# A two-layer attention trunk on one core: PSUM reads ordered behind a bank's matmuls, query halves placed by transfers, and a new issue order

## The chip, the core and the metric

The kernel runs on one core of one Trainium2 chip. Its engines run side by side, each through its own list of instructions in order: TensorE (PE, with its weight loads shown apart as PEld) multiplies matrices into PSUM, VectorE (DVE) and ScalarE (ACT) work element by element and can read PSUM, GpSimd (POOL) takes small powers, and SyncE (SP) issues the transfers. The metric is the time of one execution on the device in microseconds (us); smaller is better.

## The reference, cut to what matters

Two decoder layers over 512 tokens of width 1024, in float32. Layer 0 runs two attentions beside each other; layer 1 two others. After each layer a gated embedding is added.

```python
for i in range(2):
    h = _rms_norm(x, norm_gain[i])
    if i == 0:
        aq, ak, av, iq, ik, iw, ag, bq, bk, bv, bg = _split(h @ w_in, EVEN_SPLITS)
        # A: an indexer scores all causal keys (iq, ik, iw), each query keeps the best 128
        #    and attends to them with 8 heads (aq) on one key head
        # B: window of 128 keys, 8 heads (bq) on 2 key heads, a learned sink per head
        y = concat([attend_A * silu(ag), attend_B * silu(bg)]) @ w_out
    else:
        cq, ck, cv, cg, dq, dk, dv, dg = _split(h @ w_in, ODD_SPLITS)
        # C: dilated attention, D: difference of two softmax maps with an RMS norm per head
        y = concat([attend_C * silu(cg), attend_D * silu(dg)]) @ w_out
    x = x + y
    gate = sigmoid(_rms_norm(x, ple_norm_gain[i]) @ w_ple_gate[i])
    x = x + (p[i] @ w_ple_proj[i]) * gate
```

Queries and keys are normalised per head and rotated (`iq` is rotated only).

## The kernel before

**Products in two parts.** A float32 product is made of three matmuls on rounded parts (`PASSES`): high by high, high by low, low by high. `hilo` makes the parts: a cast on ACT writes the high part, a subtraction on DVE the low part. Weights come by a transfer into one of four `raw` buffers and are split into one of eight `w2` buffers (`weights`, `split_w`). `proj_tok` runs a projection: 8 pieces of 128 input rows, 3 passes, 4 tiles of 128 tokens, each tile into a PSUM bank of its own (`mm`, four banks). `evacuate` then empties the banks.

**Queries of layer 0.** `head_evac` scales and rotates a tile of queries, turns it with four transposes into the bank `tk`, and `put_stacked` writes it to two tensors. Even heads lie in partitions 0 to 63 of the turned bank and odd heads in 64 to 127. The first tensor holds the even heads, the high part in the lower half and the low part in the upper half of the partitions; the second holds the odd heads, with the halves the other way round. So one matmul over 128 rows takes both parts of a query at once. `put_stacked` runs for three tiles of the indexer's queries `iq` (the first needs none) and four each of `bq` and `aq`.

**Attention of layer 0.** `scores` multiplies a query tile with the keys, `exp_rows` adds the mask, finds the row's extreme on DVE and exponentiates on ACT. `attend_four` handles four heads of one query tile. Its probabilities are turned (`probs_t`) and multiplied with the values into the one bank `ob`, a column block of 128 for each head; `put_y` then reads the bank in two halves of partitions, two column blocks each, on ACT (or DVE, where the gate is multiplied in at once). `select` keeps the best 128 keys by repeated maxima on DVE.

**Layer 1.** `attend_d` collects the four heads of one query tile in the bank `ob`, and `finish_d` takes the square of each head's block on ACT, one instruction a head, before it scales the whole bank on DVE.

**The order.** The instructions aren't issued in the order in which the code names them. `Program.add` collects them with a price (`_price`) and with what each depends on: earlier instructions that touch the same part of a tile, columns of a bank in PSUM included (`_region`). `order` then runs through an imagined time, with a latency from engine to engine (`LATENCY`), and on each engine always takes the ready instruction of the lowest rank. The rank is the place in the code less a lead; `LEADS` lists a lead for each call of a decorated function (`@nc.part`). Transfers are priced by their bytes, in one queue. `issue` writes the instructions in the order that results.

In the profile every instruction stands under line 273, the call in `issue`; so tiles tell the groups apart. A name such as `ob<-pt,Ve` gives what is written and what is read. `slot` stands for all large tensors, queries and keys and the gated outputs among them; `sk` is a bank of scores, `tk` a bank of transposes, `pr` a row of probabilities, `pt` the turned ones, `pw` the stored product of the embedding, `t` a scratch tile and `tiny` a small one.

Of the kernel before, what the change touches and what calls it, by code (L numbers as in the profile page):

```python
# [21 lines left out]
P = 128  # L22
# [9 lines left out]
    "att": (34, -15, -766, -398, 669, 588, -77, -21, 2, 2, -149, -357, 50, 0, 7, 0, -82, -39, -2, 0, 30, 15, 0, 3,  # L32
# [6 lines left out]
    "idx": (1, -20, -4),  # L39
    "mm": (-20, 10, 0, -43, 0, -64, 152, 90, 1, 224, 32, -17, 67, -92, -33, -44, -226, 0, -5, 55, -26, -29, 207, -105,  # L40
         -78, 0, -70, -24, 0, -1013),
    "norm": (54, -1, 44, 0, 0, 0, 3, -51, 184, -234, 155, -150, -144, 161, 0, -203, 12, -2, -4, -232, 186, -87, 0, 0),
    "rows": (88, -835),
    "ss": (212, 408, 29, -8, 332, 193, 0, -1, -40, 0, -36, 98, 3, -61, 0, 337, 0, 2, 0, 33, 172, -17, -59, 3, 106, 28,
         378, -8, -232, 0, 0, -90),
    "tab": (880, -60, 139, -139, -289, -486),
    "top": (1, 0, -372, -1080, 138, -26, -16, -711, 22, -43, -305, -1922),
    "w": (-3, 80, 32, 111, -1, 0, 135, 10, 450, -45, -94, 0, -49, 0, -1, 13, -7, 0, 299, -31, -34, -26, 20, 32, 0, -1,
         0, 31, 9, 123),
    "x": (-355, 29),  # L50
    "y": (-697, -48, -1871, 13, 52, 122, 0, 3, -51, 11, 306, 0, -35, 6, -396, 0),
    None: 53,
# [4 lines left out]
SWITCH = 200  # L57
PR = 8
TOPK = 128
# [17 lines left out]
class Program:  # L77
# [9 lines left out]
    def _kept(ap):  # L87
# [5 lines left out]
               ("vector", "gpsimd"): 165, ("scalar", "gpsimd"): 185, ("vector", "vector"): 125, ("scalar", "scalar"): 140,  # L93
# [33 lines left out]
    def _price(self, engine, method, reads, writes):  # L127
        n = max([self._elements(x) for x in writes] + [self._elements(x) for x in reads if x.space != DRAM] + [1])
        if method == "dma_start":
            return 450  # L130
        if engine == "gpsimd":
            if n > 8:
                return 156 + 2.2 * n
            return 400 + 172 * n if method == "tensor_tensor" else 450
        psum = any(x.space == PSUM for x in reads)
        half = writes[0].ap[0][1] == 64
        pointers = sum(self._elements(x) == 1 for x in reads) if n > 1 else 0
        if engine == "scalar":
            return (58 if psum else 98) + 0.834 * n + 93 * (pointers + len(writes) - 1) + 122 * half
        if engine == "vector":  # L140
            fast = method == "tensor_scalar" and not psum
            return 72 + (0.52 if fast else 1.042) * n + 61 * pointers + 97 * half + 62 * (method == "match_replace")
        n = self._elements(writes[0])
        if method == "transpose":
            return 109
        if reads[0].dtype == BF16:
            return 427
        if reads[0].dtype == F32R:
            return max(109, 0.455 * n)
        return 218 / 128 * n  # L150
# [10 lines left out]
    def add(self, engine, method, args, kw):  # L161
# [22 lines left out]
        found = [(self._region(x), w) for w, xs in ((False, reads), (True, writes)) for x in xs]  # L184
        for (name, p0, p1, at), w in found:
            for j, v, q0, q1, there in self.touched.setdefault(name, []):
                if (w or v) and p0 < q1 and q0 < p1 and not at.isdisjoint(there):
                    after.add(j)
# [88 lines left out]
def tile_trunk(ctx: ExitStack, tc: tile.TileContext, a: dict, out: bass.AP):  # L277
# [123 lines left out]
    def proj_tok(pieces_n, evac, tiles=range(NT), order="kt", act=None, swap=0, cut=False):  # L401
# [5 lines left out]
        def mms(t, i, c0=0, c1=n):  # L407
            kt, w2 = pieces[i]
            for c, (xa, wa) in enumerate(PASSES):
                nc.tensor.matmul(banks[t][:, c0:c1], act[kt ^ (4 * swap)][:, xa, t * P:(t + 1) * P], w2[:, wa, c0:c1],  # L410
                                 start=(i == 0 and c == 0), stop=(i == last and c == 2))
        if order == "kt":
            for t in tiles:
                banks[t] = mm_bank()
            for i in range(last + 1):
                for t in tiles:
                    mms(t, i)
# [132 lines left out]
    def put_stacked(dst, t, bank):  # L550

        bv = bank.rearrange("p (k n) -> p k n", k=4)
        for j, d in enumerate(dst):
            own, other = [slice(64 * i, 64 * i + 64) for i in (j, 1 - j)]
            d = d[:, :, t * P:(t + 1) * P]
            hilo(d[own], d[other], bv[own])
# [86 lines left out]
    def attend_four(qb, key0, qT, kv, g, V, mask, y0, sink=None):  # L643
        nkb = qb + 1 - key0
        n = nkb * P
        nm, den, r = [tiny(4, tag=x, bufs=3) for x in ("nm", "den", "r")]
# [7 lines left out]
        if sink is not None:  # L654
            es = tiny(4, tag="es", bufs=3)
# [146 lines left out]
    proj_tok(wiq, head_evac(iqT, (cs, sn), rs0, normed=False, put=put_stacked), tiles=(1, 2, 3))  # L802
# [314 lines left out]
```

## Time and profile before

| | us |
|---|---|
| median of 3 runs | 685.43 |
| lowest and highest | 685.33, 685.48 |
| profiled execution | 685.89 |
| its span, first to last instruction | 684.1 |
| TensorE busy | 672.8 |
| DVE busy | 521.5 |
| ACT busy | 424.9 |
| POOL busy | 69.9 |

The span is that of the profiled execution; the time around it (1.8 us) is the rest of that execution. Busy times are sums over the span. Matmuls are pipelined and their ends are modelled, so TensorE's busy time includes part of its short waits.

### The profile page before, as it was taken

The numbers are of one execution on the slowest core, as the hardware profiler recorded it, in microseconds if no ns is written. First come the engines' busy times: TensorE is split into PE (matmuls) and PEld (weight loads), VectorE is DVE, ScalarE is ACT, GpSimd is POOL, SyncE is SP. The second block draws the span as 40 slices with busy tenths as digits, with TensorE's granted clock in tenths as the row PEclk, the third lists the DMA queues.
The fourth block names the chain that finished last, engine by engine and source line by source line (L and its number), as shares of the span: only waits on it lengthen the run. The fifth ranks groups of instructions, "written<-read, shape, count | busy, mean of one in ns | idle before, by whom it ended". The sixth has DMA issues, their size and how long they took to land.

```text
span 684.1 us, 10327 instructions
## 1 busy us (share of the span) xinstructions
PE 672.8 (98%) x3494; PEld 542.6 (79%) x3494; DVE 521.5 (76%) x1236; ACT 424.9 (62%) x968; POOL 69.9 (10%) x55
## 2 busy tenths in 40 slices
PE   9999999999999999999999999999999999999997
PEld 5888787788888888888778877777887877788886
DVE  6799999999998954554479389988699688755462
ACT  6767588889897763445456256767467565664341
POOL 0120221000010000100123031001141000000000
PEclk9999999999999999999999999999999999999999
DMA  9714131535221332232443322113024034132231
GB/s 334 290 46 139 47 93 45 159 92 164 98 63 32 121 115 74 78 130 95 131 130 114 96 62 78 47 61 108 17 77 144 13 109 138 47 106 64 77 124 46
DMA packets 37652, 68.45 MB, mean 100 GB/s; under 512 B 5216, under 2 KB 6624, under 8 KB 37344
## 3 DMA queue, kind: packets, MB, share of 16 engines
q1 hardware_dynamic: 37456, 67.79, 31.2%
q8 instruction: 27, 0.44, 0.3%
q14 instruction: 25, 0.20, 0.1%
q10 hardware_dynamic: 144, 0.02, 0.0%
HBM read 61.49 MB, written 6.30 MB: 99 GB/s over the span
## 4 chain that ended last, share of the span: by engine, by line
PE 89%; ACT 4%; DVE 3%; DMA 2%; issue 1%; SPq 0%; ACTq 0%; DVEq 0%
PE mm L273 68%; PE ob L273 8%; PE sk L273 8%; PE tk L273 6%; ACT pr L273 1%; DMA raw<-in_w_in_odd_dram 1%; DVE t L273 1%; DVE slot L273 1%; ACT slot L273 1%; DMA slot<-in_xT_dram 1%; ACT w L273 1%; DVE w L273 1%; DMA raw<-in_w_in_even_dram 0%; ACT t L273 0%; ACT pt L273 0%
## 5 line engine op out<-in xcount | busy, mean ns | idle before, releaser
L273 PE MATMUL mm<-w,AT 128*128 128x512 f32 (+2 forms) x1728 | 433.3, 398 | 0.4 <-DVE w L273 0.3
L273 PEld LDWEIGHTS mm<-w,AT 128*128 128x128 f32 x1728 | 312.2, 188 | 67.9 <-DVE w L273 1.6
L273 PE MATMUL mm<-AT,w 128*128 128x512 f32 x384 | 105.4, 405 | 0.0
L273 ACT ACTIVATE w<-raw,gains 128x512 fp32r<-128x512 f32 x96 | 67.8, 721 | 50.1 <-PE mm L273 41.4
L273 POOL TENSOR_TENSOR tiny<-tiny,mhalf 128x8 f32<-128x8 f32 (+1 forms) x32 | 59.5, 1864 | 372.1 <-DVE tiny L273 371.5
L273 DVE SCALAR_TENSOR_TENSOR w<-raw,gains,w 128x512 fp32r<-128x512 f32 x96 | 70.3, 746 | 34.5 <-ACT w L273 34.2
L273 PEld LDWEIGHTS mm<-AT,w 128*128 128x128 f32 x384 | 68.1, 189 | 12.8 <-issue 0.9
L273 ACT ACTIVATE pr<-pr,nm 128x256 f32<-128x256 f32 (+3 forms) x128 | 68.6, 538 | 15.5 <-DVE nm L273 15.1
L273 ACT CAST w<-raw 128x512 fp32r<-128x512 f32 x79 | 47.5, 619 | 22.6 <-PE mm L273 17.2
L273 PE MATMUL sk<-slot,slot 128*128 128x256 f32 (+7 forms) x368 | 61.1, 332 | 0.1
L273 DVE TENSOR_TENSOR w<-raw,w 128x512 fp32r<-128x512 f32 x80 | 54.2, 683 | 8.3 <-ACT w L273 8.2
L273 PEld LDWEIGHTS sk<-slot,slot 64*128 64x128 f32 (+1 forms) x368 | 42.9, 187 | 15.1 <-issue 3.6
L273 PE MATMUL tk<-ident,pr 128*128 128x128 f32 x256 | 44.7, 275 | 0.1
L273 PE MATMUL ob<-pt,Ve 128*128 128x128 f32 x272 | 39.6, 280 | 3.0 <-ACT slot L273 2.3
L273 PEld LDWEIGHTS ob<-pt,Ve 128*128 128x128 f32 x272 | 35.0, 191 | 8.8 <-ACT pt L273 3.6
L273 ACT CAST slot<-tk 64x512 fp32r<-64x512 f32 (+1 forms) x42 | 24.5, 583 | 23.2 <-PE tk L273 22.1
L273 DVE CUSTOM_DVE_ANT_0 pr<-sk,cpack 128x128 f32<-128x128 f32 (+3 forms) x72 | 31.5, 461 | 7.8 <-PE sk L273 7.5
L273 PEld LDWEIGHTS tk<-ident,pr 128*128 128x128 f32 x256 | 31.3, 141 | 7.5 <-ACT pr L273 1.4
L273 ACT COPY pt<-tk 128x512 f32<-128x512 f32 (+3 forms) x56 | 27.4, 490 | 13.0 <-PE tk L273 12.5
L273 DVE TENSOR_TENSOR t<-raww,tab 128x512 f32<-128x512 f32 x48 | 32.1, 681 | 4.0 <-ACT raww L273 3.8
L273 DVE TENSOR_TENSOR slot<-slot,mm 128x512 f32<-128x512 f32 x32 | 21.3, 684 | 16.3 <-PE mm L273 16.2
L273 DVE SCALAR_TENSOR_TENSOR t<-t,slot 128x512 f32<-128x512 f32 (+1 forms) x17 | 11.2, 659 | 29.3 <-ACT t L273 29.3
(98 smaller groups left out, 787.0 us busy)
## 6 DMA issues: line engine op xcount, KB each, us to landing
raw<-in_w_in_odd_dram SPq DMA_DIRECT2D x64, 256.0 KB, 2.7
raw<-in_w_in_even_dram SPq DMA_DIRECT2D x36, 256.0 KB, 3.1
raw<-in_w_ple_gate_dram SPq DMA_DIRECT2D x32, 256.0 KB, 3.0
slot<-in_x_dram SPq DMA_DIRECT2D x16, 256.0 KB, 6.3
raw<-in_w_out_even_dram SPq DMA_DIRECT2D x16, 256.0 KB, 2.8
raw<-in_w_out_odd_dram SPq DMA_DIRECT2D x16, 256.0 KB, 2.6
raw<-in_w_ple_proj_dram SPq DMA_DIRECT2D x8, 256.0 KB, 2.8
pw<-t SPq DMA_DIRECT2D x8, 256.0 KB, 3.5
```

Of the source, the lines that this page charges most:

```text
L273: getattr(getattr(nc, engine), method)(*args, **kw)
```

## The change

- **Reads of PSUM** (`Program.add`): an instruction of any engine but TensorE that touches a PSUM tile counts as touching all of it. Before, only the columns and partitions that it names counted.
- **Queries of layer 0** (`put_stacked`): the high and the low part of a tile are made on all 128 partitions at once, in two new buffers `qh` and `ql` (two each); four transfers, each of 64 partitions, carry the halves to their places.
- **First piece** (`proj_tok(..., first=True)`, used for `iq`): for the first piece of weights the passes run over all tiles in turn, and the pass with the weights' low part comes last.
- **Prices**: a power on POOL 500 + 185 n ns instead of 400 + 172 n, the latency from DVE to POOL 400 instead of 165 ns, a matmul 0.456 instead of 0.455 ns a column.
- **Buffers**: the small tiles `nm`, `den`, `r` and `es` of `attend_four` are two deep instead of three.
- **Order**: all entries of `LEADS` are new (cut here).

```diff
@@ -29,33 +29,36 @@
 BIG = 1.0e30
 GONE = -3.0e38
 LEADS = {
...
-    None: 53,
+    None: 62,
 }
 VECS = ("a_q_gain", "a_k_gain", "idx_k_gain", "b_q_gain", "b_k_gain", "c_q_gain", "c_k_gain", "d_q_gain", "d_k_gain",
         "d_lambda_q1", "d_lambda_k1", "d_lambda_q2", "d_lambda_k2")
 CPACK = 1792
 SWITCH = 200
+WHOLE = frozenset(range(512))
 PR = 8
+QB = 2
 TOPK = 128
 IDX_SCALE = 512.0 ** -0.5
 LAMBDA_INIT = 0.8 - 0.6 * math.exp(-0.3)
@@ -90,7 +93,7 @@
     ENGINES = ("tensor", "vector", "scalar", "gpsimd", "sync")
     LATENCY = {("scalar", "vector"): 140, ("scalar", "tensor"): 160, ("vector", "scalar"): 125, ("vector", "tensor"): 170,
                ("tensor", "scalar"): 210, ("tensor", "vector"): 215, ("gpsimd", "vector"): 80, ("gpsimd", "scalar"): 90,
-               ("vector", "gpsimd"): 165, ("scalar", "gpsimd"): 185, ("vector", "vector"): 125, ("scalar", "scalar"): 140,
+               ("vector", "gpsimd"): 400, ("scalar", "gpsimd"): 185, ("vector", "vector"): 125, ("scalar", "scalar"): 140,
                ("gpsimd", "gpsimd"): 120, ("tensor", "tensor"): 0}
 
     def __init__(self, tc):
@@ -131,7 +134,7 @@
         if engine == "gpsimd":
             if n > 8:
                 return 156 + 2.2 * n
-            return 400 + 172 * n if method == "tensor_tensor" else 450
+            return 500 + 185 * n if method == "tensor_tensor" else 450
         psum = any(x.space == PSUM for x in reads)
         half = writes[0].ap[0][1] == 64
         pointers = sum(self._elements(x) == 1 for x in reads) if n > 1 else 0
@@ -146,7 +149,7 @@
         if reads[0].dtype == BF16:
             return 427
         if reads[0].dtype == F32R:
-            return max(109, 0.455 * n)
+            return max(109, 0.456 * n)
         return 218 / 128 * n
 
     @contextmanager
@@ -182,6 +185,8 @@
             self.extra[i] = 7000 if any(list(x.ap)[-1][1] == 1 or list(x.ap)[-1][0] > 1 for _, x in aps) else 0
         after = self.after[i]
         found = [(self._region(x), w) for w, xs in ((False, reads), (True, writes)) for x in xs]
+        if engine != "tensor":
+            found = [((r[0], 0, P, WHOLE), w) if x.space == PSUM else (r, w) for (r, w), x in zip(found, reads + writes)]
         for (name, p0, p1, at), w in found:
             for j, v, q0, q1, there in self.touched.setdefault(name, []):
                 if (w or v) and p0 < q1 and q0 < p1 and not at.isdisjoint(there):
@@ -398,15 +403,16 @@
         evac(t, bank, *columns)
 
     @nc.part("mm")
-    def proj_tok(pieces_n, evac, tiles=range(NT), order="kt", act=None, swap=0, cut=False):
+    def proj_tok(pieces_n, evac, tiles=range(NT), order="kt", act=None, swap=0, cut=False, first=False):
         pieces, n = pieces_n
         act = [AT[:, :, kt, :] for kt in range(NK)] if act is None else act
         banks = {}
         last = len(pieces) - 1
 
-        def mms(t, i, c0=0, c1=n):
+        def mms(t, i, c0=0, c1=n, passes=range(3)):
             kt, w2 = pieces[i]
-            for c, (xa, wa) in enumerate(PASSES):
+            for c in passes:
+                xa, wa = PASSES[c]
                 nc.tensor.matmul(banks[t][:, c0:c1], act[kt ^ (4 * swap)][:, xa, t * P:(t + 1) * P], w2[:, wa, c0:c1],
                                  start=(i == 0 and c == 0), stop=(i == last and c == 2))
         if order == "kt":
@@ -414,7 +420,12 @@
                 banks[t] = mm_bank()
             for i in range(last + 1):
                 for t in tiles:
-                    mms(t, i)
+                    if i or not first:
+                        mms(t, i)
+                if first and not i:
+                    for c in (0, 2, 1):
+                        for t in tiles:
+                            mms(t, i, passes=(c,))
             for t in tiles:
                 evacuate(evac, t, banks[t])
         else:
@@ -549,11 +560,13 @@
 
     def put_stacked(dst, t, bank):
 
-        bv = bank.rearrange("p (k n) -> p k n", k=4)
+        hi, lo = [sb.tile([P, 4, P], F32R, name=uid(x), tag=x, bufs=QB) for x in ("qh", "ql")]
+        hilo(hi, lo, bank.rearrange("p (k n) -> p k n", k=4))
         for j, d in enumerate(dst):
             own, other = [slice(64 * i, 64 * i + 64) for i in (j, 1 - j)]
             d = d[:, :, t * P:(t + 1) * P]
-            hilo(d[own], d[other], bv[own])
+            nc.sync.dma_start(out=d[own].bitcast(F32), in_=hi[own].bitcast(F32))
+            nc.sync.dma_start(out=d[other].bitcast(F32), in_=lo[own].bitcast(F32))
 
     def head_evac(dst, tab, rs, normed=True, put=put_heads):
         def evac(t, bank):
@@ -643,7 +656,7 @@
     def attend_four(qb, key0, qT, kv, g, V, mask, y0, sink=None):
         nkb = qb + 1 - key0
         n = nkb * P
-        nm, den, r = [tiny(4, tag=x, bufs=3) for x in ("nm", "den", "r")]
+        nm, den, r = [tiny(4, tag=x, bufs=2) for x in ("nm", "den", "r")]
         prs = []
         for p in (2 * g, 2 * g + 1):
             for j, bank in enumerate(scores(qT, kTe, p, qb, key0, n, kv)):
@@ -652,7 +665,7 @@
                 init = 3.0e38 if sink is None else sink[0][:, h:h + 1]
                 prs.append(exp_rows(bank, n, mask[:, :n], init, nm[:, i:i + 1], den[:, i:i + 1]))
         if sink is not None:
-            es = tiny(4, tag="es", bufs=3)
+            es = tiny(4, tag="es", bufs=2)
             nc.vector.tensor_tensor(out=es, in0=nm, in1=sink[1][:, 4 * g:4 * g + 4], op=ALU.add)
             nc.scalar.activation(out=es, in_=es, func=AF.Exp)
             nc.vector.tensor_tensor(out=den, in0=den, in1=es, op=ALU.add)
@@ -799,7 +812,7 @@
         norm_scale(t, rs0)
 
     iqT = heads()
-    proj_tok(wiq, head_evac(iqT, (cs, sn), rs0, normed=False, put=put_stacked), tiles=(1, 2, 3))
+    proj_tok(wiq, head_evac(iqT, (cs, sn), rs0, normed=False, put=put_stacked), tiles=(1, 2, 3), first=True)
     wsmall = split_w(([(kt, wsm[kt // 4][:, kt % 4, :456]) for kt in range(NK)], 456))
     ktab = slot([P, 4, T]).rearrange("p a (b h d) -> p (a b) h d", b=2, h=4).rearrange("p (u t) h d -> p u t h d", u=2)
     for i, (gname, sc) in enumerate((("a_k_gain", 8.0), ("idx_k_gain", 8.0 * IDX_SCALE), ("b_k_gain", 8.0),
```

## Rows read from the trace of the kernel before

**Rows 1.** The page, busy time of each engine, share of the span and instructions.

```profile
PE 672.8 (98%) x3494; PEld 542.6 (79%) x3494; DVE 521.5 (76%) x1236; ACT 424.9 (62%) x968; POOL 69.9 (10%) x55
```

**Rows 2.** Busy time by stretch: length, then each engine's us, granted clock, transfers.

```profile
75.00:135.00 60.00, 58.89 (x317) 47.65 (x316) 57.44 (x158) 48.02 (x118) 12.48 (x6) 1.00 0.32 93
135.00:200.00 65.00, 64.45 (x385) 54.09 (x384) 63.28 (x199) 57.45 (x160) 3.96 (x2) 1.00 0.34 106
...
240.00:320.00 80.00, 79.36 (x402) 64.80 (x401) 40.73 (x71) 37.80 (x75) 2.74 (x5) 1.00 0.31 99
```

**Rows 3.** The bank `ob`: who waited for it, us in total, times.

```profile
PEld ob L273: 5.7, 9
...
PE ob L273: 3.9, 8
```

**Rows 4.** The timeline of `ob`: start, length, instruction, [idle before it, releaser].

```profile
95.13 1.05 PE L273 MATMUL ob<-pt,Ve 128*128 128x128 f32 x8
...
109.31 0.94 PE L273 MATMUL ob<-pt,Ve 128*128 128x128 f32 x6
...
110.28 0.38 ACT L273 ACTIVATE slot<-ob 64x256 f32<-64x256 f32 x1 [0.49 <-PE ob L273]
...
110.72 0.49 PE L273 MATMUL ob<-pt,Ve 128*128 128x128 f32 x2 [0.47 <-ACT slot L273]
...
578.59 0.61 PE L273 MATMUL ob<-slot,pt 128*128 128x128 f32 x4
...
579.74 0.49 PE L273 MATMUL ob<-slot,pt 128*128 128x128 f32 x2 [0.55 <-ACT t L273]
```

**Rows 5.** Groups by shape: count, busy us, mean ns, idle before.

```profile
L273 DVE TENSOR_TENSOR slot<-tk,slot 64x512 fp32r<-64x512 f32 x22 | 15.2, 689 | 4.8 <-ACT slot L273 4.4
...
L273 DVE TENSOR_TENSOR slot<-tk,slot 128x512 fp32r<-128x512 f32 x20 | 13.7, 683 | 0.8 <-ACT slot L273 0.7
...
L273 ACT CAST slot<-tk 64x512 fp32r<-64x512 f32 x22 | 12.8, 581 | 5.9 <-PE tk L273 4.9 <-DVE slot L273 0.8
...
L273 ACT CAST slot<-tk 128x512 fp32r<-128x512 f32 x20 | 11.7, 586 | 17.2 <-PE tk L273 17.2
```

**Rows 6.** The timeline near 119 us: a query's second cast, matmuls of an embedding product.

```profile
119.07 0.58 ACT L273 CAST slot<-tk 64x512 fp32r<-64x512 f32 x1 [0.80 <-DVE slot L273]
...
120.32 0.97 PE L273 MATMUL mm<-w,w 128*128 128x512 f32 x3 [0.63 <-ACT t L273]
```

**Rows 7.** The timeline of two query tiles and of the scores that follow.

```profile
40.41 1.39 DVE L273 TENSOR_TENSOR slot<-tk,slot 64x512 fp32r<-64x512 f32 x2 [0.24 <-ACT slot L273]
...
54.12 0.40 PE L273 MATMUL sk<-slot,slot 128*128 128x256 f32 x2
...
84.31 1.18 ACT L273 CAST slot<-tk 64x512 fp32r<-64x512 f32 x2 [2.46 <-PE tk L273]
...
85.52 1.41 DVE L273 TENSOR_TENSOR slot<-tk,slot 64x512 fp32r<-64x512 f32 x2 [0.33 <-ACT slot L273]
...
86.26 0.51 PE L273 MATMUL sk<-slot,slot 128*128 128x256 f32 x2
```

**Rows 8.** Transfers by kind (KB each, median us to landing), and one issue.

```profile
pw<-t SPq DMA_DIRECT2D x8, 256.0 KB, 3.5
...
out_dram<-slot SPq DMA_DIRECT2D x2, 128.0 KB, 1.8
...
124.63 0.39 SPq L273 DMA_DIRECT2D pw<-t  x1
```

**Rows 9.** The timeline of SP's queue: eight weight loads.

```profile
53.61 22.54 SPq L273 DMA_DIRECT2D raw<-in_w_in_even_dram  x8
```

**Rows 10.** The timeline of TensorE at the start.

```profile
6.07 1.47 PEld L273 LDWEIGHTS mm<-w,AT 128*128 128x128 f32 x7 [0.35 <-DVE w L273]
...
10.58 2.60 PE L273 MATMUL mm<-w,AT 128*128 128x512 f32 x10 [0.30 <-DVE w L273]
```

**Rows 11.** Groups by shape: the powers on POOL.

```profile
L273 POOL TENSOR_TENSOR tiny<-tiny,mhalf 128x8 f32<-128x8 f32 x24 | 50.8, 2121 | 280.8 <-DVE tiny L273 280.8
```

More of the change, by code (lines that the diff above doesn't have):

```diff
@@ L31 @@
 LEADS = {
-    "att": (34, -15, -766, -398, 669, 588, -77, -21, 2, 2, -149, -357, 50, 0, 7, 0, -82, -39, -2, 0, 30, 15, 0, 3,
[6 rows of a table removed]
[L39 to L51, printed above, removed]
-    None: 53,
+    "att": (-392, -476, -265, 55, 575, -382, 44, 15, -6, -149, -341, -446, -4, -57, 63, -14, 2, 2, -287, 388, 0, 0,
[7 rows of a table added]
+    "idx": (-5, -2, 0),
+    "mm": (15, 0, 153, 0, 10, -336, -84, 2, 8, 4, 0, -30, 30, -5, 88, -12, -304, 0, 41, 13, 136, -25, 206, -141, -135,
+         -6, -996, -1930, -2303, -10383),
+    "norm": (-3, -2, 0, -170, 60, -38, 0, -13, 142, 15, 0, -227, 0, -49, 15, -1, 0, 0, -396, -7, 21, 0, 0, -1844),
+    "rows": (0, 898),
+    "ss": (-64, 0, 0, 340, 576, 4, -39, 1269, 0, 0, -74, 119, 196, 55, 333, 112, -4, 45, -250, -182, 70, 0, 0, 1, 14,
+         -119, 0, 74, 0, 1, 0, -88),
+    "tab": (279, 13, -4, 0, -137, -2),
+    "top": (193, -101, -908, -1349, 180, 58, -8, -21, -2, 3, -1659, -1846),
+    "w": (-57, 169, 413, -21, 0, -44, -172, 0, 3, 0, -2, 1, -44, 74, -2, -20, -89, 234, 3, 68, -363, 0, 0, -80, -19,
+         0, -19, 0, -854, -1336),
+    "x": (2, 0),
+    "y": (825, 483, 0, -2, -20, 0, 0, -16, 32, 4, 0, 202, 1, -123, -517, -335),
+    None: 62,
 }
```

13 rows, old and new, of the table LEADS are left out of this document.

## The prediction

> **What bounds the kernel now.** I read the page's busy times first: TensorE is busy for 98% of the span [rows 1]. So the span is a queue of matmuls in one order, and time can come only from two places: gaps in that queue, and stretches where something else feeds it too slowly. The table by stage shows which engine is next [rows 2]. From 75 to 200 us, the attention of layer 0 among its projections, DVE works 57.44 of 60 and 63.28 of 65 us (96% and 97%) beside TensorE; from 240 to 320 us, the end of layer 0, it works 40.73 of 80. The granted clock is 1.00 in all of them, so the clock is no part of this case. The reader is to see two near-bounds in layer 0 and one bound after it.
>
> The page hides short gaps, because a matmul's modelled end covers part of a wait. So I looked at the weight loads (PEld) and at the bank `ob`, which collects the attention output. Its view names the waits [rows 3]: the loads for matmuls into `ob` sat idle 5.7 us in 9 waits, the matmuls 3.9 us in 8. The timeline shows what they are [rows 4]. A group of eight matmuls into `ob` normally runs through in 1.05 us. At 109.31 six of the eight run; ACT then reads part of the bank at 110.28 for 0.38 us; the last two start at 110.72, released by that read. The two matmuls write other columns than the read touches, so nothing in the arithmetic asks for this wait: the read was issued ahead of two matmuls of its own group, and the bank is then handed back and forth. In layer 1 the same happens with the squares of `finish_d`: four matmuls, a square, and the next matmul only at 579.74. I count eight such places: six in `attend_four` (near 110, 183, 204, 212, 221 and 252 us, the last with DVE as reader) and two in `attend_d` (580 and 595).
>
> **The change part by part.**
>
> *Reads behind all matmuls of a bank.* In `add`, a read of PSUM by another engine than TensorE now counts as a read of the whole bank. It therefore follows every matmul that the program wrote into that bank before it, and since `order` appends a call only after all that it depends on, the read stands behind them in the issued order too. An issued order of that kind cannot give the wait of [rows 4]. Its price: the loads' 5.7 us. From the other side, the group at 109.31 ends at 110.72 + 0.49 = 111.21, 1.90 us after its start, against 1.05 undisturbed: 0.85 longer, six times 5.1. At 578.59 six matmuls take until 579.74 + 0.49, 1.64 us, where eight undisturbed take 1.05: at least 0.59 longer, twice 1.2. Together 6.3, somewhat too much, since a little of the 0.85 lies ahead of the read. Bounds 3.9 (the matmuls' own idle) and 6.3; I take **-5.7**, the row between them. What is late next: the reads. In `attend_four` they now start after eight matmuls instead of six, but the pause is gone, so the bank comes free no later. In `finish_d` four squares now follow the last matmul, where up to three ran earlier, so the end of `finish_d` comes later by the length of three squares. After the last `finish_d` TensorE has the 48 matmuls of `ple_products(1)` to cover it; three like them take 0.97 us [rows 6], so they last over 10.
>
> *Natural 128-row parts.* `put_stacked` runs for 11 tiles (3 of `iq`, 4 each of `bq` and `aq`). It made two casts on 64 partitions at 581 ns and two subtractions at 689; now it makes one cast and one subtraction on 128 partitions, 586 and 683 ns [rows 5]. DVE is saved 2 x 0.689 - 0.683 = 0.695 us a tile, 7.6 in all; ACT 0.576 a tile, 6.3 in all. How much is on the path? The three `iq` tiles lie before the crowded stretch. The other eight free 8 x 0.695 = 5.6 us of DVE, which is the upper bound if DVE alone paced 75 to 240 us; the lower is 0, if TensorE did. One place shows the halves in the way directly [rows 6]: the second cast waits 0.80 us for the subtraction of the first half, the copy that empties a product bank is queued behind it on ACT, and TensorE stands 0.63 us for that copy. I take that place and a little more, **-1.0**, nearer to the lower end because TensorE is still busy 58.89 of those 60 us [rows 2].
>
> *Transfers.* Each tile now needs four transfers of 64 partitions x 512 (128 KB), 44 in all on SP's queue. Today a tile is ready 86.93 - 84.31 = 2.62 us after its first cast, and the first scores start 0.67 us before that, with the first half [rows 7]. New path: 0.59 + 0.1 + 0.68 = 1.4 us to the parts, three more issues ahead of the last transfer at 0.33 to 0.39 each = 1.1, and a landing between 1.8 us (128 KB to DRAM) and 3.5 us (256 KB from SBUF) [rows 8]. That is 4.3 to 6.0 us, so a tile is 1.7 to 3.4 us later. For `iq` this costs nothing: the last put ends at 41.80 and the first score starts at 54.12 [rows 7]. Of the other eight, four have their first score within a microsecond of the put (86.26 is one; the others lie near 101, 176 and 215 us); four have 2 us or more. So the cost lies between 0 (other projections stand in the matmul queue there and fill in) and 4 x 3.4 = 13.6. The order counts each transfer at 1.3 us after the queue and its bytes, and gives it 256 KB instead of 128, so it places scores late enough; I take **+1.0**, four tenths of one tile missed at 2.5, the middle of 1.7 and 3.4. The transfers also stand in line with the weight loads on SP, each of which waits for a buffer that DVE's splits free; eight loads spread over 22.54 us at 53.61 [rows 9]. The new buffers `qh` and `ql` are two deep and puts of every second tile lie 10 us or more apart at the start and around 105 us, so they add no wait. `nm`, `den`, `r`, `es` two deep instead of three cost 0: a call of `attend_four` takes four of the eight `pr` buffers, so two calls are in flight at most already.
>
> By the Trainium skill, "SBUF — State Buffer", section "Door 1: The DMA port swizzle", a transfer on 64 partitions reaches only half of SBUF's ports (196 GB/s) and two transfers on the two halves of the partitions go one after the other, which speaks against four 64-row transfers. As an estimate from that page, four would take 4 x 131 KB / 196 GB/s = 2.7 us and some 2 us fixed, 6.1 us from the cast with the 1.4 above; no run here shows it yet. By it a missed tile would cost 6.1 - 2.62 = 3.5 us instead of 2.5, and the term would be +1.4, the sum -5.5.
>
> *First piece of weights.* `first=True` sends the matmuls with the low part of the first weights to the end of that piece; the loads wait 0.35 us for that part at 6.07. The next waits there are for later pieces, 0.30 us at 10.58 [rows 10], so most of what is saved is waited for again: **-0.2**, between 0 and -0.35.
>
> *POOL's prices.* An 8-column power took 2121 ns [rows 11]; the formula gave 400 + 172 x 8 = 1776 and now gives 500 + 185 x 8 = 1980. The list of waits has no entry of DVE, ACT or TensorE behind such a power, so this is 0, and so is 0.456 for 0.455.
>
> *The order.* All LEADS are new. No row prices that; a new order can remove or recreate waits of the size of [rows 4]. Four either way at 0.7 is **0, with +-3**.
>
> **Sum.** -5.7 - 1.0 + 1.0 - 0.2 = -5.9. The profiled execution took 685.89 us (span 684.1 and 1.8 around it); it would take 680.0. The median of the runs shown is 685.43, 0.46 below the profiled one: 679.5.
>
> **The rivals.**
> *Late queries (slower).* The four tiles that come just in time find no cover. Place: TensorE's first scores after a put in `attend_b` and `attend_a`, behind transfers that wait in SP's queue for a weight load ahead of them. A load spacing of 22.54/8 = 2.8 us comes on top of the later landing. Against: TensorE has projections to do there. Price: 2.8 + 2.5 = 5.3 us an uncovered tile; it decides from the second tile on (10.6 > 6.9 gained otherwise). With two, 685.4 - 6.9 + 10.6 = 689.1. Chance 0.15.
> *DVE is the bound of layer 0.* Then the five `attend_four` waits between 110 and 221 us are slack that DVE's pace takes back, and 8 x 0.695 is not found either, because the order spends it. Only 252, 580 and 595 stay: -0.85 - 1.2 = -2.1, 683.3. For: 96 and 97%. Against: DVE's relief is in the same stretch. Chance 0.12.
> *Both bounds fall.* The waits and DVE's whole relief count: -5.7 - 5.6 - 0.2 = -11.5, 673.9. Chance 0.06.
> *The reads do move, but the new order gives it back.* -5.9 + 6 or so: within 0.2% of before. Chance 0.08.
>
> **How the numbers follow.** My forecast has 0.59: 676.5 to 682.5 with the order's +-3 alone. 0.2% is 1.4 us, about what a measurement of this kernel can tell from no change. Faster: 0.59 + 0.06, and 0.09 of DVE's 0.12 = 0.74. Within 0.2%: 0.08 and the other 0.03 = 0.11. Slower 0.15. The range runs from 674.5, inside the case where both fall, to 686.0; above it lie the late queries and part of the case of no change, some 0.17, below it 0.04.
>
> **What would show it.** Right: the view of `ob` names no load or matmul behind an ACT or DVE read inside a group, every group of eight runs in about 1.05 us; 11 casts and 11 subtractions on 128 rows in place of 22 and 22; the table by stage shows DVE 5 to 7 us less up to 240 us. Wrong: score loads that wait for a transfer, by more than 2 us in total; weight splits that wait for `raw` where they do not today; or as much TensorE time up to 240 us with the `ob` waits gone, which would make DVE the bound.

## The result, and the profile after

The changed kernel took 676.7 us (median of 4 runs, 676.1 to 677.4) against 685.4 for the kernel before, measured beside it (685.0 to 685.5): a ratio of 0.9873, 95% interval 0.9861 to 0.9884, or 8.7 us less. The profiled execution took 677.39 with a span of 675.6.

The page's row of busy times answers to [rows 1]:

```profile
PE 668.0 (99%) x3494; PEld 543.9 (81%) x3494; DVE 513.7 (76%) x1225; ACT 415.4 (61%) x957; POOL 68.7 (10%) x55
```

DVE works 7.8 us less and ACT 9.5; TensorE, with the same 3494 matmuls, is "busy" 4.8 us less. So more than half of the 8.5 us that the span lost had stood as busy time on the page of before; the likely reason is that a modelled end covers a stall. The stretches of [rows 2] in the changed kernel, with the same columns:

```profile
75.00:135.00 60.00, 60.00 (x337) 50.38 (x336) 59.64 (x166) 48.60 (x122) 12.20 (x6) 1.00 0.51 139
135.00:200.00 65.00, 65.00 (x418) 57.76 (x417) 64.28 (x200) 59.15 (x168) 3.65 (x2) 1.00 0.38 115
240.00:320.00 80.00, 80.00 (x368) 64.44 (x367) 41.67 (x71) 35.36 (x70) 4.18 (x6) 1.00 0.32 100
```

TensorE has no idle left in them, and the first two hold more matmuls than before (337 for 317, 418 for 385). DVE is no freer in them than it was: the work that it lost was replaced by work from later on. Only over the whole stretch from 0 to 240 us is it busy 4.8 us less, 216.4 instead of 221.2.

Where the time came from is read from a milestone, the transfers that keep the result of layer 0 (`xkept`): the view of that tile, before and then after, with count, ns and the start of the first and the last.

```profile
L273 SPq DMA_DIRECT2D xkept<-slot x8: 319/326/327, 287.3 to 332.3; - x8
```
```profile
L278 SPq DMA_DIRECT2D xkept<-slot x8: 319/327/807, 278.5 to 321.4; - x8
```

From the first of them to the end of the span it is 684.1 - 287.3 = 396.8 us before and 675.6 - 278.5 = 397.1 after. The whole gain lies in layer 0; layer 1 gave nothing. A new wait there, on the timeline near 554 us, takes part of what its two places of [rows 4] give back:

```profile
553.17 0.62 ACT L278 CAST w<-raw 128x512 fp32r<-128x512 f32 x1 [1.94 <-DMA raw<-in_w_out_odd_dram]
553.70 0.37 ACT L278 COPY pt<-tk 128x256 f32<-128x256 f32 x1
...
554.11 0.71 PE L278 MATMUL ob<-slot,pt 128*128 128x128 f32 x4 [0.82 <-ACT pt L278]
```

ACT waits for a weight, the copy that TensorE needs is queued behind it, and TensorE stands 0.82 us.

The bank `ob`, who waited, answers to [rows 3]:

```profile
  ACT slot L278: 4.5, 5
  DVE slot L278: 3.9, 4
...
  ACT t L278: 1.9, 3
```

No load of `ob` and no matmul of it stands there any more; only ACT and DVE wait there. Groups run whole, as at 118.41 here (TensorE's timeline, to compare with [rows 4]):

```profile
118.41 1.05 PE L278 MATMUL ob<-pt,Ve 128*128 128x128 f32 x8
```

The casts and subtractions by shape, to be set against [rows 5], and the new transfers (KB each, median us to landing):

```profile
L278 DVE TENSOR_TENSOR ql<-tk,qh 128x512 fp32r<-128x512 f32 x11 | 7.5, 685 | 0.4 <-ACT qh L278 0.3
...
L278 ACT CAST qh<-tk 128x512 fp32r<-128x512 f32 x11 | 6.4, 586 | 5.8 <-PE tk L278 5.7
```
```profile
slot<-qh SPq DMA_DIRECT2D x22, 128.0 KB, 2.4
slot<-ql SPq DMA_DIRECT2D x22, 128.0 KB, 2.5
```

One tile's way, from the timeline between 83 and 94 us, and the transfer rate from 85 to 95 us in 40 slices of 0.25 us:

```profile
87.13 0.59 ACT L278 CAST qh<-tk 128x512 fp32r<-128x512 f32 x1 [1.54 <-PE tk L278]
87.75 1.26 SPq L278 DMA_DIRECT2D slot<-qh  x2
87.84 0.69 DVE L278 TENSOR_TENSOR ql<-tk,qh 128x512 fp32r<-128x512 f32 x1
89.06 1.29 SPq L278 DMA_DIRECT2D slot<-ql  x2
...
91.81 0.42 PEld L278 LDWEIGHTS sk<-slot,slot 128*128 128x128 f32 x2
...
92.51 0.42 PEld L278 LDWEIGHTS sk<-slot,slot 128*128 128x128 f32 x2
```
```profile
GB/s 0 0 0 0 0 0 0 0 0 0 0 0 0 0 0 0 160 180 176 234 176 211 199 182 219 180 168 12 0 0 57 82 188 393 309 193 211 205 246 275
```

The four transfers move their bytes from 89.0 to about 91.8 us. The load at 91.81 takes the first of the two tensors, with no wait for a transfer: 4.68 us after the cast's start, where the first scores of [rows 7] came 86.26 - 84.31 = 1.95 after it. The load at 92.51 takes the second. By the trace the last transfer of the first tensor had landed at 91.50 and that of the second at 92.15, so the order places the scores 0.3 to 0.4 us behind the landing.

### The profile page after: what moved, and what is told of

It reads as the page before. It is cut to its first block, busy times and chain, and to the rows that moved or that the text cites. A ratio compares the mean times of both kernels' runs of the same rounds, so it can differ in the third digit from the quotient of the medians.

```text
span 675.6 us, 10378 instructions
## 1 busy us (share of the span) xinstructions
PE 668.0 (99%) x3494; PEld 543.9 (81%) x3494; DVE 513.7 (76%) x1225; ACT 415.4 (61%) x957; POOL 68.7 (10%) x55
## 4 chain that ended last, share of the span: by engine, by line
PE 92%; DMA 3%; DVE 2%; ACT 1%; issue 1%; SPq 0%; DVEq 0%; ACTq 0%
PE mm L278 70%; PE sk L278 8%; PE ob L278 7%; PE tk L278 6%; DMA raw<-in_w_in_odd_dram 2%; DMA slot<-in_xT_dram 1%; DVE t L278 1%; DMA raw<-in_w_out_odd_dram 1%; DVE w L278 1%; ACT w L278 0%; DVE AT L278 0%; ACT t L278 0%; DVE slot L278 0%; SPq L278 0%; DVE tiny L278 0%
## 5 line engine op out<-in xcount | busy, mean ns | idle before, releaser
L278 POOL TENSOR_TENSOR tiny<-tiny,mhalf 128x8 f32<-128x8 f32 (+1 forms) x32 | 56.9, 1780 | 351.2 <-DVE tiny L278 351.2
L278 PE MATMUL sk<-slot,slot 128*128 128x256 f32 (+7 forms) x368 | 64.6, 330 | 0.0
L278 DVE TENSOR_TENSOR w<-raw,w 128x512 fp32r<-128x512 f32 x80 | 53.8, 682 | 14.0 <-ACT w L278 13.6
L278 PE MATMUL ob<-pt,Ve 128*128 128x128 f32 x272 | 37.2, 276 | 0.0
L278 ACT ACTIVATE t<-mm,rsn 128x512 f32<-128x512 f32 (+1 forms) x17 | 11.0, 662 | 40.0 <-PE mm L278 40.0
L278 POOL TENSOR_TENSOR rsn<-tiny,mhalf 128x1 f32<-128x1 f32 x16 | 11.3, 710 | 215.6 <-DVE tiny L278 215.5
```

The source lines that it names most:

```text
L278: getattr(getattr(nc, engine), method)(*args, **kw)
```

## The experiments

Each run was measured beside the kernel before, and the third column is the difference of the two medians. The last column is the difference of two such differences.

| run | us | against before | ratio, 95% interval | against after |
|---|---|---|---|---|
| changed kernel | 676.7 | -8.7 | 0.9861 to 0.9884 | |
| before_reads_behind | 682.64 | -2.4 | 0.9954 to 0.9979 | |
| before_relief | 682.21 | -3.0 | 0.9946 to 0.9974 | |
| before_relief_reads | 678.66 | -6.6 | 0.9893 to 0.9920 | |
| before_put_kept | 696.53 | +11.5 | 1.0152 to 1.0196 | |
| after_reads_ahead | 690.31 | +5.3 | 1.0061 to 1.0088 | +13.9 |
| after_put_halves | 687.39 | +2.3 | 1.0024 to 1.0049 | +11.0 |
| after_sub2 | 683.41 | -1.8 | 0.9968 to 0.9985 | +6.9 |
| after_dma2 | 767.44 | +82.2 | 1.1182 to 1.1223 | +90.9 |
| after_old_order | 686.29 | +1.4 | 1.0006 to 1.0041 | +10.1 |
| after_no_first | 675.51 | -9.4 | 0.9854 to 0.9881 | -0.7 |
| after_spare_transfers | 689.92 | +5.0 | 1.0057 to 1.0084 | +13.7 |
| after_spare_behind | 686.33 | +1.2 | 1.0006 to 1.0039 | +9.9 |

Except in after_old_order (and four rows of after_no_first) TensorE's matmuls stand in the order of the kernel that each was made from.

**The reads alone, in the old order.** `order` runs as before; then each reader of a bank is moved behind all matmuls that the program wrote into it earlier.

```diff
+            self.whole[i] = {j for x in reads if x.space == PSUM for j in self.wrote[x.tensor.name]}
...
-            for i in self.order():
+            out = self.order()
+            for i, behind in self.whole.items():
+                self.after[i] |= behind
+            for i in self.behind(out):
```

> The kernel before with its own order; only the 16 reads of the bank ob that stood ahead of matmuls of their own group (7 in attend_four, 9 squares) are issued behind the last of them. Matmuls, DVE, POOL and SP keep their order. If TensorE's queue sets the pace, the eight waits of the prediction go and the time falls by 5.7 us, to about 679.7 (ratio 0.992). If DVE sets the pace of layer 0, only the waits near 252, 580 and 595 us count: -2.1, 683.3 (0.997).

It gained 2.4, between 1.4 and 3.2. The waits of the weight loads from 25 to 260 us (total, times, longest), before and then here, show why it is not 5.7:

```profile
PEld ob L273 <- ACT slot L273: 3.3, 5, 0.7
...
PEld tk L273 <- ACT pr L273: 1.4, 6, 0.5
PEld sk L273 <- DVE nm L273: 1.2, 5, 0.4
PEld sk L273 <- DVE slot L273: 1.2, 4, 0.4
PEld tk L273 <- ACT pt L273: 0.8, 3, 0.4
...
PEld ob L273 <- DVE slot L273: 0.7, 1, 0.7
```
```profile
PEld tk L294 <- ACT pr L294: 2.3, 7, 0.6
PEld sk L294 <- DVE slot L294: 2.1, 5, 0.9
PEld sk L294 <- DVE nm L294: 2.0, 8, 0.4
...
PEld tk L294 <- ACT pt L294: 1.6, 4, 0.8
```

The 3.3 + 0.7 us for `ob` are gone, and all rows of the answer still sum to 18.3, as before (18.2): the loads came earlier to the next point where DVE or ACT was late. The -2.1 of the rival with DVE as the bound is close in size, but not in place, as the milestone says:

```profile
L294 SPq DMA_DIRECT2D xkept<-slot x8: 319/326/327, 284.7 to 329.6; - x8
```

Of the 2.8 us that the span lost, 287.3 - 284.7 = 2.6 lie in layer 0. From there to the end it took 681.3 - 284.7 = 396.6 us, where it took 396.8 before; the rival had put 1.2 of its 2.1 there.

**The natural parts alone, and with the reads.** In the old order, one cast and one subtraction on 128 rows in place of the halves, straight into the two tensors and without transfers, so that the halves of the queries stand in the wrong places; then the same with the reads behind.

```diff
+            for i, (hi, lo), bv in self.halves:
+                self.calls[i][1][:] = [("copy", (), dict(out=hi, in_=bv))]
+                self.calls[i + 1][1][:] = [("tensor_tensor", (), dict(out=lo, in0=bv, in1=hi.bitcast(F32), op=ALU.subtract))]
+                for j in (i + 2, i + 3):
+                    self.calls[j][1].clear()
...
```

> The kernel before with its own order; put_stacked makes one cast into the first tensor and one subtraction into the second, on 128 partitions, and leaves out the placing of the halves (no transfers; the queries of layer 0 stand in the wrong halves). So DVE has 7.6 us and ACT 6.3 us less, and no query is later. If DVE paces layer 0, the time falls by 4 to 5.6 us, to 679.5 to 681. If the order of the changed kernel brought its gain, by 1 or less, 684 or more.

> As before_relief (the placing of the halves left out), and the 16 reads of the bank ob behind their matmuls too. The reads alone gave 2.4 us. If DVE's pace is what swallowed the rest of their 5.7, the two together give more than the sum of each alone: 8 to 10 us, 675 to 677, as much as the whole change. If the order is what matters, 3 to 4 us, 681 to 682.

The relief alone gave 3.0, not 1.0. Together they gave 6.6, where 2.4 + 3.0 = 5.4; the 1.2 more is within what the three intervals leave open, and neither forecast (8 to 10, or 3 to 4) holds it. The loads' waits from 25 to 260 us sum to 8.7 us with both, against 18.3 with the reads alone, so less is waited for again. From 25 to 260 us TensorE was busy 231.08 of 235 us before (1288 matmuls), 232.79 with the reads behind (1296), 231.66 with the relief (1301), 234.28 with both (1320), and 235.00 (1332) in the changed kernel.

**The transfers, in the old order.** The kernel before with natural parts and the 44 transfers; the four of a tile are issued where its first subtraction stood. The rest of the order is as it was, the small tiles are two deep.

```diff
+                    hi, lo = parts[first]
+                    nc.vector.tensor_tensor(out=lo, in0=bv, in1=hi.bitcast(F32), op=ALU.subtract)
+                    for j, d in enumerate(dst):
...
+                        nc.sync.dma_start(out=d[own].bitcast(F32), in_=hi[own].bitcast(F32))
+                        nc.sync.dma_start(out=d[other].bitcast(F32), in_=lo[own].bitcast(F32))
```

> The kernel before with its own order of matmuls; in put_stacked alone one cast, one subtraction and four transfers stand where the two casts and two subtractions stood (small tiles two deep, to make room). Nothing is fitted to the later landing. If queries are late where the scores come just in time, four tiles cost 1.7 to 3.4 us each: +6 to +13 less about 1 for the shorter casts, 690 to 697, with waits of the score loads for transfers. If DVE's pace is what counts, 5 us of it or more come back and the time falls to about 681. If neither counts, 685.

It lost 11.5, so beside before_relief the transfers cost 14.5. TensorE's timeline names them at four places:

```profile
87.09 0.47 PE L295 MATMUL sk<-slot,slot 128*128 128x256 f32 x2 [2.12 <-DMA slot<-ql]
105.71 0.41 PE L295 MATMUL sk<-slot,slot 128*128 128x128 f32 x2 [2.12 <-DMA slot<-ql]
...
148.98 0.51 PE L295 MATMUL sk<-slot,slot 128*128 128x256 f32 x2 [1.52 <-DVE nm L295]
183.20 0.47 PE L295 MATMUL sk<-slot,slot 128*128 128x256 f32 x2 [1.94 <-DMA slot<-ql]
184.62 0.48 PE L295 MATMUL sk<-slot,slot 128*128 128x256 f32 x2 [0.48 <-DMA slot<-ql]
...
225.07 0.71 PE L295 MATMUL sk<-slot,slot 128*128 128x512 f32 x2 [1.60 <-DMA slot<-ql]
```

These are the four tiles that the prediction had named as just in time, in the same sequence, 2.12 + 2.12 + 1.94 + 0.48 + 1.60 = 8.3 us together; the tile near 183 us has two of the waits. (The weight loads show waits at the same moments; they are the same stalls and aren't added.) The rest of the 14.5 isn't a query that lands late. One part is a weight: ACT's cast of one waits 4.40 us for its transfer at 145.09, and TensorE stands 1.52 soon after, at 148.98, behind DVE, which had waited for ACT. Another is the clock, 0.87 from 80 to 90 us and 0.96 from 90 to 100, where before_relief has 1.00: 10 x 0.13 + 10 x 0.04 = 1.7. Some 3 us I can't assign.

**The reads, undone in the changed kernel.** 25 readers of `ob` (16 in `attend_four`, 9 squares) pulled ahead of the matmuls that they don't need.

```diff
+            for j, spare in self.spare.items():
+                if j not in done and not spare <= done and self.after[j] - spare <= done:
+                    done.add(j)
+                    placed.append(j)
```

> The changed kernel with its own order; 25 reads of the bank ob (16 halves in attend_four, 9 squares in finish_d) are issued as soon as the matmuls that they need have been issued, ahead of the rest of their group. If each costs TensorE the 0.7 us that such a wait cost before, 14 to 18 us more, 691 to 695. If DVE's pace hides those of layer 0, only the squares and two more count: at most +8, 685.

It lost 13.9. The view of the bank `ob` shows the hand-overs back:

```profile
  PEld ob L298: 12.3, 18
...
  PE ob L298: 9.0, 19
```

The first `xkept` came at 287.6 of a span of 688.1, so 9.1 us went in layer 0 and 400.5 - 397.1 = 3.4 in layer 1: some 0.57 us for each of the 16, 0.38 for each of the 9.

**The halves put back, and the subtraction doubled.** First the changed kernel with two casts and two subtractions on 64 partitions a tile and no transfers; then with each of the 11 subtractions done twice (7.5 us more of DVE).

```diff
+                self.calls[i][1][:], self.calls[i + 1][1][:] = casts, subs
```
```diff
         hilo(hi, lo, bank.rearrange("p (k n) -> p k n", k=4))
+        nc.calls[-1][1].append(nc.calls[-1][1][0])
```

> The changed kernel with its own order of matmuls; put_stacked alone is as it was: two casts and two subtractions on 64 partitions in the place of one each, no transfers. DVE works 7.6 us more and ACT 6.3. If DVE paces layer 0, +4 to +7 us (681 to 684). If TensorE's queue does, the queries come earlier and only a few short waits appear: 0 to +1.5 (677 to 678).

> The changed kernel, same order; each of the 11 subtractions of put_stacked is issued twice, so DVE works 7.5 us more and ACT nothing. If DVE's work alone paces layer 0, +5 to +7.5 us (682 to 684). If TensorE's queue paces it now, under +1.5. If the 10.7 us of after_put_halves came from the changing between ACT and DVE, or from ACT, also little, under +4.

The halves cost 11.0, more than the 4 to 7 expected, and the doubled subtractions 6.9: for these 0.9 us of time for each microsecond of DVE. At that rate DVE's 7.6 us make 7 of the 11.0. The other 4 came with 6.3 us more of ACT and with casts and subtractions that take turns: from 75 to 135 us DVE waits 1.8 us for casts of queries, where in the changed kernel it waits for none. No run parts the two. From 75 to 135 us, with the halves and then doubled:

```profile
75.00:135.00 60.00, 55.70 (x288) 42.95 (x287) 57.78 (x148) 45.09 (x106) 11.59 (x6) 1.00 0.19 59
```
```profile
75.00:135.00 60.00, 57.62 (x311) 46.35 (x310) 59.61 (x160) 43.91 (x107) 11.60 (x6) 1.00 0.46 122
```

Doubled, DVE is at 99% and TensorE falls to 311 matmuls from 337. In this stretch DVE and TensorE bind together: what is added to DVE is nearly all added to the program.

**Each transfer twice, to the same place.**

```diff
             nc.sync.dma_start(out=d[own].bitcast(F32), in_=hi[own].bitcast(F32))
+            nc.calls[-1][1].append(nc.calls[-1][1][0])
```

> The changed kernel, same order; each of the 44 transfers of put_stacked is issued twice in a row, so a tile's last transfer comes four issues, 2.4 us, later and SP issues 26 us more. If the new order covers the landing with room to spare, 0 to +1 (676.7 to 677.7). If it is fitted to the edge, tiles come late: +4 us or more, with score loads that wait for transfers.

This measured something else: the second transfer waits on SP until the first has landed, 84.6 us in all, and the weight loads stand behind it.

```profile
SPq L278 <- DMA slot<-qh: 44.5, 22, 6.0
...
SPq L278 <- DMA slot<-ql: 40.1, 22, 2.5
```

The loss of 90.9 is near that sum, though not the same microseconds: TensorE's granted clock fell as well, to 0.76 from 50 to 100 us. It tells of waits in SP's queue and not of the cover behind a landing.

**More transfers without that wait.** Beside the 44, as many into a spare tensor: one ahead of each, then four behind each tile's four.

```diff
+                nc.calls[-1][1].insert(0, ("dma_start", (), {"out": spare, "in_": x[own].bitcast(F32)}))
```
```diff
+            nc.calls[-1][1].append(("dma_start", (), {"out": spare, "in_": x[own].bitcast(F32)}))
```

> The changed kernel; ahead of each of the 44 transfers of query halves stands one more of the same size, into a spare tensor in DRAM that nothing reads, so that the four of a tile are issued 0.6 to 2.4 us later and the transfers of this kind are twice as many. Every engine's own order is unchanged. It asks how much cover the new order leaves behind the landing. Theory (the order leaves about 2 to 3 us, since no score load waits for a transfer in the changed kernel's trace): 0 to +3, so 676.7 to 680. Rival (the order is fitted to the landing to within a microsecond): eight tiles of bq and aq lose up to 2.4 us each, at least four of them, so +6 to +19, 683 to 696.

> As after_spare_transfers, with the four spare transfers of a tile behind its four real ones instead of one ahead of each. A tile's own transfers are then issued when they were, and only what follows them in SP's queue comes 2.4 us later, the weight loads above all. It tells apart what cost the 13 us there. Theory A (weight loads behind the transfers: in that run TensorE stood 4.25 us near 50 us behind a weight that landed 4.6 us late for its cast): most of it stays, +8 to +13, 685 to 690, with ACT's casts of weights waiting for transfers and the waits for slot<-ql gone. Theory B (the later landing of the queries): 0 to +4, 676.7 to 681.

Ahead they cost 13.7, behind 9.9. With the spares ahead the list of waits (25 to 330 us) has both causes (PE and PEld wait at the same moments here too):

```profile
ACT w L278 <- DMA raw<-in_w_in_even_dram: 6.9, 4, 4.6
PE sk L278 <- DMA slot<-ql: 3.5, 4, 1.4
PEld sk L278 <- DMA slot<-ql: 2.6, 2, 1.8
```

With the spares behind, no wait for a query's transfer is left, and the weights' stay (3.1 us for layer 0's input weights in the changed kernel):

```profile
ACT w L278 <- DMA raw<-in_w_in_even_dram: 8.3, 4, 3.0
ACT w L278 <- DMA raw<-in_w_ple_proj_dram: 3.2, 2, 1.9
```

So the larger part of the loss comes with weight loads that stand behind the transfers. Whether they wait in SP's queue or while the bytes ahead of them move, no run parts; layer 0's input weights took 3.5 us from issue to landing from 25 to 240 us (median), 3.0 in the changed kernel. The landing has little cover either, as the 0.3 to 0.4 us above say.

**The old leads on the new code.** All code of the changed kernel, `LEADS` of before.

> All code of the changed kernel with the leads of the kernel before, so that the order is not fitted to the transfers, the longer reads and the freed DVE. Theory (the fit of the order hides the landing of the transfers): the runs so far price the reads and the natural parts together at -6.6 without any transfer (678.66) and the transfers in an order not made for them at +11.5; the sum is 685.2 - 6.6 + 11.5 = 690, between 686 and 696, with several us of score loads that wait for slot<-qh or slot<-ql. Rival (the planner, which knows the transfers' price, hides them with any leads, and the new leads are worth only the +-3 of my prediction): 677 to 681, with under 2 us of such waits.

686.3 (684.0 to 689.9), so on the new code the new leads are worth 10.1 beside the old ones; on the old code they weren't tried. Of that little is transfers; TensorE's matmuls wait for one at a single place up to 290 us:

```profile
182.07 0.47 PE L277 MATMUL sk<-slot,slot 128*128 128x256 f32 x2 [1.43 <-DMA slot<-ql]
```

The time is the theory's, the mechanism the rival's: a planner that knows a transfer's price keeps nearly all scores behind the landing with these leads too (1.4 us against 8.3 above). What the leads bring is that DVE's and ACT's work is ready in time as well: the loads' waits from 25 to 260 us sum to 14.1 us here and to 3.8 in the changed kernel, and the largest of the 14.1 are for `pt` (2.5), `t` (2.5) and `nm` (2.0).

**Without `first`.**

```diff
-    proj_tok(wiq, head_evac(iqT, (cs, sn), rs0, normed=False, put=put_stacked), tiles=(1, 2, 3), first=True)
+    proj_tok(wiq, head_evac(iqT, (cs, sn), rs0, normed=False, put=put_stacked), tiles=(1, 2, 3))
```

> The changed kernel with the passes of the first piece of weights in their old order; four rows of TensorE's order differ, the other engines' are the same. Theory of the prediction (first is worth -0.2, between 0 and -0.35): 676.7 to 677.1. Rival (at the start another transfer or split is waited for in any case): 676.7, no difference that five rounds show.

675.5; the two intervals overlap almost wholly, so no gain from `first` is shown. What sets the start is another thing, as TensorE's timeline of the changed kernel says, to compare with [rows 10]:

```profile
10.70 0.50 PE L278 MATMUL mm<-w,AT 128*128 128x512 f32 x1 [0.64 <-ACT w L278]
11.63 10.76 PE L278 MATMUL mm<-w,AT 128*128 128x512 f32 x45 [0.43 <-DVE w L278]
```

The wait for the first low part is gone, but a later one is longer, and the unbroken run starts at 11.63 instead of 10.58. In the run without `first` it starts at 5.07 with no gap in the matmuls at all. How late the first transfers land differs by more than the 0.2 in question: ACT's first casts of the input wait 2.8 us for them in the changed kernel's trace, 1.5 in the other.

## Why the prediction was right, and where its terms were not

The reads, the natural parts and the transfers work as the prediction says, and the sum came out 2.8 us short; 676.7 lies near the lower end of the likeliest case's own range (676.5 to 682.5). That the sum is so near is partly luck: its terms were off in both directions and made up for each other. Of its signs, the `ob` waits are gone, the groups run whole, there are 11 casts and 11 subtractions, and no score load waits for a transfer. DVE's 4.8 us less up to 240 us is just under the 5 to 7 given.

- **What bounds the kernel.** Right about TensorE and DVE in layer 0. Not drawn from it: where two engines bind together, removing a wait of the one is repaid only as far as the other can follow.
- **Reads, -5.7.** The mechanism is shown: the `ob` waits vanish with the reads moved, alone and in the changed kernel, and return when they are pulled ahead. The size was wrong: -2.4 alone, because TensorE came earlier to the next point where DVE or ACT was late. The two places of layer 1, priced at 1.2, gave next to nothing with the reads alone (396.8 to 396.6) and nothing in the changed kernel (397.1).
- **Natural parts, -1.0.** DVE's 7.6 us less was right (7.8 on the page). I took a value near the lower bound because TensorE was busy 98% of the stretch; the runs gave -3.0 alone, and -4.2 on top of the reads (6.6 - 2.4). A TensorE that is "busy" 98% by modelled ends did not speak against DVE. What ACT's 6.3 us less had to do with it, no run shows apart.
- **Transfers, +1.0.** A tile now takes 4.68 us from its cast to its scores, inside the 4.3 to 6.0. An issue took 0.63 us instead of 0.33 to 0.39. "The order places scores late enough" was right. Without it four tiles miss, the four named, by 1.6 to 2.4 us each, 2.1 on average; the term had 1.7 to 3.4. The price is 14.5 all the same, a little above my upper bound of 13.6: weights come later too, and a pause cost clock. Neither was in the term, and some 3 us stay open.
- **The order, 0 with +-3.** The mis-sized term that matters most. On the new code the new leads are worth 10.1. In the changed kernel no score load waits for a transfer, and it ends 2.1 us below the run with reads and relief that has no transfers at all (8.7 - 6.6).
- **`first` -0.2 and POOL's prices 0.** The first is too small to be seen here. The second wasn't tried by itself, since new prices change the whole order; nor was the depth of the small tiles.
- **The rivals.** DVE as the bound has the size of the reads in the old order (-2.1 forecast, -2.4 measured), but by luck: it had put 1.2 of it into layer 1, where 0.2 came. "Both bounds fall" has the direction in which the sum was short. Late queries happened where the transfers met an order not made for them; of the load ahead of them in SP's queue that the rival reckoned with, the runs show the reverse, weights behind the transfers.

By the Trainium skill, "SBUF — State Buffer", section "Door 1: The DMA port swizzle", a 64-partition transfer reaches half of the ports; the page gives 196 GB/s for it, measured at 1 MiB. This trace agrees: 160 to 234 GB/s, 190 on average, in the eleven slices of the four transfers, while with a weight load of 128 partitions among them it comes to 393 a little later. The estimate of 6.1 us from the cast that I made from that page was too long; the last of the four landed 5.0 us after the start of the cast, since issue, subtraction and transfer overlap.

## What to carry to other kernels

When two engines are each over 95% busy in a stretch, don't price a removed wait of the one at its full length: the 5.7 us here gave 2.4. Reads and relief together gave 6.6, and 8.7 with an order made for both. A hidden step keeps its price: the transfers, which no score load waits for here, cost 14.5 us in the old order, and queries come late, or weights behind them do, as soon as something is added. Take the time of a stretch from milestones and counts of matmuls in a window, not from TensorE's busy share, which counted more than half of this gain as work.

## What the runs showed of the hardware

**An issue of these transfers took SP longer than that of a weight load.** The `slot<-qh` above took 1.26 us for two, while the next weight load of 128 partitions and twice the bytes took 0.34 (SP's timeline of the changed kernel):

```profile
91.63 0.34 SPq L278 DMA_DIRECT2D raw<-in_w_ple_proj_dram  x1
```

The two differ in partitions, in the length of their pieces (512 bytes against 2 KB) and in where they read, and no run shows which of these counts.

**A pause of TensorE can be paid for again in clock.** With the spare transfers ahead, TensorE stood 4.25 us near 50 us, behind the cast of a weight that came 4.6 us late. Its timeline, and the stretch 50 to 60 us (columns as in [rows 2]):

```profile
47.61 2.73 PE L278 MATMUL mm<-w,AT 128*128 128x512 f32 x11
54.59 1.09 PE L278 MATMUL tk<-ident,t 128*128 128x128 f32 x4 [4.25 <-DVE tiny L278]
55.33 1.20 PE L278 MATMUL mm<-w,AT 128*128 128x512 f32 x2
```
```profile
50.00:60.00 10.00, 5.75 (x19) 4.60 (x18) 6.21 (x13) 4.65 (x9) 1.11 (x1) 0.66 0.72 208
```

Eleven matmuls took 2.73 us before the pause and two took 1.20 behind it; the granted clock of the stretch is 0.66, a mixture of the levels of 2.4 and 1.2 GHz, where every stretch of the changed kernel from 20 to 320 us has 1.00. So part of the 13.7 us of that run is clock, which none of my expectations had. Not every pause is followed by it: in before_put_kept the clock fell behind the pause of 2.12 us before 87.09 (0.87 from 80 to 90 us), but not behind the equally long one before 105.71 (1.00 from 100 to 120).
